# Moving four accumulations into x forward in the gated end stage of a transformer trunk, and one weight split ahead of a product's gating

## The chip, the cores and the metric

The kernel runs on one core of one Trainium2 chip. The metric is device time in microseconds (us) of one execution; the median over the runs shown is what counts.

## The reference, cut to what matters

One layer (DEPTH is 1, so the mixer is the sliding-window attention) on x of 512 rows and 2048 columns, all in float32:

```python
hn = rmsnorm(x, norm_g[i])
y = swa_mixer(hn, swa_w_in[j], swa_w_out[j], swa_sinks[j], rel_bias)   # ends in (out * silu(gate)) @ w_out
x = x + y
emb = p[i] @ ple_proj[i]
g = jax.nn.sigmoid(rmsnorm(x, ple_norm[i]) @ ple_gate[i])
x = x + emb * g
...
return rmsnorm(x, final_g)
```

The change lies in the last four lines: the product with `ple_gate` (2048 x 2048), the sigmoid, the update of x, and the final norm of each row.

## The kernel before

A float32 product is made of three matmuls in the fast float32 format (`mm3`): each operand is split into a high part (a cast on ScalarE, ACT) and a low part (a subtraction on VectorE, DVE). For the weights of `ple_gate` the cast is `bhi` (L755) and the subtraction `blo` (L756), each over a block of 128 x 1024; for the other operand they are `fhg` (L865) and `flg` (L866). ACT and DVE split two blocks ahead of TensorE (PE), and room for the split parts is reused, so that a split also waits for PE to have finished an older block.

The product with `ple_gate` is cut into halves of rows and of columns and made with seven smaller products instead of eight, numbered 1 to 7. Six of them run in the order 1, 7, 6, 5, 3, 4 (`ORDER_PLE`); product 2 is itself made by smaller ones (`Small`). Each of the six goes over two column blocks jj = 0, 1, and each of those over four weight blocks m = 0 to 3 (`unit`); a block is 12 matmuls with 512 columns. Behind each block `some_later` issues part of a list of postponed steps (`later`), and `todo` issues what a table gives for that place, named (product, jj, block). The order on every engine in this stage is the order in which the code issues (manual schedule for PE, SP, DVE, ACT and POOL), and each engine takes its instructions strictly in that order.

Weights reach SBUF in two ways. Plain blocks `braw` are loaded by the SyncE queue (SP). The blocks of products 7, 6 and 4 share eight tiles `grown`: loaded for product 7, then twice added to in place by a DMA that accumulates, from the GpSimd queue (POOL, L734). `Pieces.get` sets when such an addition is issued: its place is entered in `due`, and before the change this was 2 weight blocks behind the use by product 7 and 6 behind the use by product 6. Product 4's eight blocks are split into their own tiles, `last` (ACT, L763) and `low` (DVE, L764), by `split_last(k)`, k = 0 to 7.

Once a sum of products is complete for a quarter of the output, it is gated (`gated`): ACT makes `s` = sigmoid(rstd * z) (L1387), DVE multiplies by the embedding `e` (L1389), the result is added to `x1s` (the 512 x 2048 x, as column blocks j of 512 and row blocks t of 128), and ACT sums the squares of the new x for the norm (L1406). For t < 2 with j < 2 (the first quarter, its values in tile `s1`) and for t >= 2 with j >= 2 (values in `s7`) the addition is a DMA that accumulates, on POOL's queue (L1393); elsewhere it is an addition on DVE (L1395). `gate_later` puts these steps on `later`; for the first quarter the four DMAs go to the list `moves` and the squares to `moved`, and the lists are emptied into `later` at set places.

Behind the fifth product (3), whose second half is gated as `two`, comes the sixth (4) as four `block`s; their PSUM banks are filled beforehand with a copy from `s2` (`open_bank`, L1480). Rows 0 to 255 are then complete: DVE sums the squares (L1599), POOL makes the root (L1361), and rows are scaled by it and by `fg`, the final gain (`row` on DVE, L1424, or a scaling on ACT, L1432, on values that `by_gain`, L1416, has multiplied before), and stored by SP. Row blocks 2 and 3 follow in the same way.

Of the kernel before, what the change touches and what calls it, by code (L numbers as in the profile page):

```python
# [55 lines left out]
def trunk_kernel(ctx: ExitStack, tc: tile.TileContext, a: dict):  # L56
    nc = tc.nc
# [24 lines left out]
    def bank(name, tag):  # L82
        return others.get(tag, psum).tile([P, 512], F32, tag=tag, name=name)
# [4 lines left out]
    class Weights:  # L88
# [24 lines left out]
        def get(self, i):  # L113
            while self.asked <= min(i + self.ahead, len(self.srcs) - 1):
                self.todo.append(partial_of(self._make, self.asked))
                self.asked += 1
            while self.todo and not (self.apart and i < len(self.made)):
                self.todo.pop(0)()
            return self.made[i]
# [38 lines left out]
    def run(gen):  # L158
        for _ in gen:
            pass  # L160
# [21 lines left out]
    kinds, g = [], 0  # L182
# [16 lines left out]
    for k in range(KC):  # L199
# [67 lines left out]
        f, e = k == 0, k == KC - 1  # L267
# [27 lines left out]
        if 3 <= k < 3 + NB:  # L295
            t = k - 3
# [104 lines left out]
    for b in range(exact, BUCKETS):  # L401
        d = np.nonzero(bk == b)[0]
        if len(d):
            lo, n = P - 1 + int(d.min()), len(d)
# [296 lines left out]
    for nm, p in SUMS:  # L701
        for q in (6, 5) if (nm, p) == ("ple_gate", 5) else (p,):
            sum_small(nm, q)
        for jj in range(2):
            for m in range(4):
                t = summed[nm, p, jj, m] = tc.dram_tile([P, WE], F32, name=f"{nm}_{p}_{jj}_{m}")
# [13 lines left out]
    class Pieces:  # L720
# [59 lines left out]
        def get(self, i):  # L780
            self.ahead(i)

            key = self.specs[i][2]
            if key is not None:
                n = next((n for n in range(i + 1, len(self.specs)) if self.specs[n][2] == key), None)
                if n is not None:
                    self.due.append((i + (2 if self.specs[i][0] == "seed" else 6), n))
                    self.due.sort()
            while self.due and self.due[0][0] <= i:
                self._prepare(self.due.pop(0)[1])  # L790
            return self.made.pop(i)
# [177 lines left out]
    x1 = [x1s[:, j] for j in range(4)]  # L969
# [15 lines left out]
    later = []  # L985
# [6 lines left out]
    def unit(p, jj, at, forms, todo, between=lambda m, ps: None):  # L992

        ps = banks(p, jj, forms.nm)
        f = forms.made[p]
        first = p not in (6, 5, 3)
        for m in range(4):
            bh, bl = B.get(at[p, jj][m])
            for kk in range(2):
                k = 2 * m + kk  # L1000
                fh, fl = f[m]
                for tb in range(2):
                    mm3(ps[tb], fh[:, kk, blk(tb)], fl[:, kk, blk(tb)], bh[kk], bl[kk], first and k == 0, k == 7, not first)
            some_later(4 - m)
            todo()
            between(m, ps)
        return ps
# [297 lines left out]
    for n, p in enumerate(ORDER_OUT):  # L1305
        nxt = out_forms.steps(ORDER_OUT[n + 1]) if n < 5 else iter(())
        for jj in range(2):
# [28 lines left out]
            ps = unit(p, jj, at_out, out_forms, todo, between)  # L1336
# [32 lines left out]
    def load_embeds(c, jj):  # L1369
        t = embed_of[c, jj] = late.tile([P, 2, 512], F32, tag="e", name=f"e{c}_{jj}", bufs=2)  # L1370
        nc.sync.dma_start(t, embeds[c, jj])
# [40 lines left out]
    def gain(j):  # L1412
        return fg[:, j * 512 : (j + 1) * 512]

    def by_gain(t, j):
        nc.vector.tensor_mul(x1[j][:, t, :], x1[j][:, t, :], gain(j))  # L1416

    def store(t, j):
        nc.sync.dma_start(a["out"][t * P : (t + 1) * P, j * 512 : (j + 1) * 512], x1[j][:, t, :])

    def row(t, j, yn):

        xt = x1[j][:, t, :]
        nc.vector.scalar_tensor_tensor(out=xt, in0=xt, scalar=yn, in1=gain(j), op0=ALU.mult, op1=ALU.mult)  # L1424

    def rows_out(t):

        for j in (2, 3):
            row(t, j, yn2[:, t : t + 1])
            store(t, j)  # L1430
        for j in range(2):
            nc.scalar.mul(x1[j][:, t, :], x1[j][:, t, :], yn2[:, t : t + 1])  # L1432
            store(t, j)

    turns = [(kp, 1) for kp in range(4)]

    def gate(p, jj, ps, e):

        zs = []
        for tb in range(2):  # L1440
            v1, v2, v7 = s1[:, jj, tb], s2[:, jj, tb], s7[:, jj, tb]
            if p == 1:
                nc.scalar.mul(v1, ps[tb], -1.0)
            elif p == 7:
                (nc.vector.tensor_copy if tb else nc.scalar.copy)(v7, ps[tb])
            elif p == 6:
                nc.vector.tensor_add(v2, ps[tb], v7)
            elif p == 5:
                nc.vector.tensor_add(v7, ps[tb], v7)
                zs.append((2 + tb, 2 + jj, v7, v7))  # L1450
            elif p == 3:
                zs.append((tb, 2 + jj, ps[tb], v1))
            else:
                zs.append((tb, jj, v1, v1))
        return [gated(*z, e[z[0]]) for z in zs]
# [11 lines left out]
    moved, moves = [], []  # L1467
# [9 lines left out]
    def open_bank(jj, tb, tag, c=slice(0, 512)):  # L1477

        ps = opened[jj, tb, c.start] = bank(f"open{jj}_{tb}_{c.start}", tag)
        nc.scalar.mul(ps[:, c], s2[:, jj, tb, c], -1.0)  # L1480
# [24 lines left out]
    for n, p in enumerate(ORDER_PLE[:-1]):  # L1505
        if n == 1:

            ctx.enter_context(
                tc.manual_schedule(
                    engines={getattr(mybir.EngineType, v) for v in ("PE", "SP", "DVE", "Activation", "Pool")}  # L1510
                )
            )
        nxt = ple_forms.steps(ORDER_PLE[n + 1])
        for jj in range(2):
            calls = iter(range(4))

            def todo():
                step = next(calls)
                k = early.get((p, jj, step))
                if (p, jj, step) in embed_loads:  # L1520
                    load_embeds(*embed_loads[p, jj, step])
                while small_due:
                    small_due.pop(0)()
                if turns:
                    turn(*turns.pop(0), "t")
                    if not turns:
                        nc.vector.tensor_reduce(ss2, ssq2, axis=AX.X, op=ALU.add)
                        run(power_of_mean(rstd2, ss2, "r2"))
                        nc.scalar.activation(ss2[:, :1], ss2[:, :1], AF.Sigmoid)
                    return  # L1530
                next(nxt, None)
                if p == 1:
                    next(nxt, None)
                if k is not None:
                    split_last(k)
                if (p, jj, step) in opens:
                    open_bank(*opens[p, jj, step])
                if (p, jj, step) in gains:
                    by_gain(*gains[p, jj, step])

            def between(m, ps):
                if (p, m) == (7, 3):
                    gate(p, jj, ps, None)
                q = ple_steps.get((p, jj, m))
                if q is not None:
                    small_ple.prepare(q)
                for q in SMALL["ple_gate"].get((p, jj), {}).get(m, ()):
                    small_ple.product(q)
                if (p, jj, m) == (6, 1, 1):
                    later.append(partial_of(gate_later, "sum", 0, None, embeds_for(1, 0)))  # L1550

            ps = unit(p, jj, at_ple, ple_forms, todo, between)
            last_two, held_e = (p, jj) == (3, 1), {}
            if not (p == 7 or last_two):
                later.insert(0, partial_of(gate_later, p, jj, ps, held_e))
            for of, which in EMBEDS.get((p, jj), ()):
                e = embeds_for(of, which)
                held_e.update(e)
                if of == 1:
                    later.insert(1, partial_of(gate_later, "sum", which, None, dict(e)))  # L1560
                    held_e.clear()
            if (p, jj) == (5, 0):
                later.extend(moves)
            elif (p, jj) in ((5, 1), (3, 0)):
                while moved:
                    later.extend(moved.pop(0))
        run(nxt)
# [16 lines left out]
        return gated(2 + tb, jj, ps[:, c], s2[:, jj, tb, c], embed_of[4, jj][:, tb], c, share)  # L1584


    two = gate(3, 1, ps, e)
    for g in two:
        next(g)
    for g in two:  # L1590
        next(g)
    load_embeds(4, 1)
    split_last(7)
    open_bank(1, 1, "s", upper)
    for g in two:
        run(g)
    yn2 = const.tile([P, 3], F32, name="yn2")
# [5 lines left out]
    g = block(0, 0)  # L1603
    run(root)
    next(g)
    next(g)
    rows_out(0)
    run(g)
    g = block(1, 0)
    next(g)  # L1610
    next(g)
    rows_out(1)
    for j in (2, 3):
        by_gain(2, j)
    run(g)
    nc.vector.tensor_reduce(ssum[:, 2:], ssq3[:, 2, :4], axis=AX.X, op=ALU.add)
    root = power_of_mean(yn2[:, 2:], ssum[:, 2:], "r4")
    next(root)
    run(root)
    for j in range(2):  # L1620
        row(2, j, yn2[:, 2:])
        store(2, j)
# [3 lines left out]
    g = block(0, 1)  # L1626
    next(g)
    next(g)
    for j in (2, 3):
        by_gain(3, j)  # L1630
    run(g)
    by_gain(3, 0)

# [1 line left out]
    g = block(1, 1, lower)  # L1635
# [3 lines left out]
    n = done[3]  # L1639
# [81 lines left out]
```

## Time and profile before

| what | value |
| --- | --- |
| median of 3 runs (lowest to highest) | 799.19 us (798.86 to 799.58) |
| profiled execution: its time, its span | 799.52 us, 797.8 us |
| PE busy | 780.2 us, 98% of the span |
| DVE busy | 613.8 us, 77% |
| ACT busy | 525.5 us, 66% |
| POOL busy | 147.3 us, 18% |
| last matmul begins | 786.14 us |
| last product's DVE work on the result begins | 787.72 us |

Times inside the execution count from the start of the span. In a row of the timeline stand start, duration, engine, line, operation, output and input, a count where several in a row were merged, and in brackets how long the engine had stood idle before and what released it.

### The profile page before, as it was taken

The page shows a single profiled execution, that of the slowest core. Times are in us where ns is not written, and L with a number is a line of the kernel's source. Part 1 is how long each engine was busy: PE and PEld are TensorE (multiplying, and loading weights), DVE is VectorE, ACT ScalarE, POOL GpSimd, SP SyncE. Part 2 cuts the span into 40 slices and gives each one's busy share as a digit, 9 for nine tenths or more (in the row PEclk, how much of TensorE's full clock was granted, in tenths as well). Part 3 has the DMA queues.
Part 4 walks back from the last instruction along what each step waited for, and adds up shares of the span by engine and source line. Part 5 has one row for each costly group of instructions (what it writes and reads, how often), then busy time and mean ns, then how long its engine had stood idle before and what let it go on. Part 6 is the DMA issues. An engine that isn't in the chain of part 4 may idle for free. (4 is left out here: it accounts for less than half of the span.)

```text
span 797.8 us, 11160 instructions
## 1 busy us (share of the span) xinstructions
PE 780.2 (98%) x3708; PEld 651.0 (82%) x3708; DVE 613.8 (77%) x1054; ACT 525.5 (66%) x1103; POOL 147.3 (18%) x270
## 2 busy tenths in 40 slices
PE   9999999999999999999999999999999999999794
PEld 8888888888888888888888888888888888888573
DVE  4556697867877697777767998877887779988676
ACT  6752677666866677666666645667778966656773
POOL 0201423140322223141222100110000012212000
PEclk9999999999999999999999999999999999999897
DMA  9988999999999989999988499776894499997725
GB/s 350 283 225 270 210 287 299 277 290 246 294 280 273 259 227 297 249 313 232 307 240 187 162 351 335 232 223 241 310 354 163 165 334 275 272 302 235 211 73 192
DMA packets 49961, 205.94 MB, mean 258 GB/s; under 512 B 7456, under 2 KB 8480, under 8 KB 44144
## 3 DMA queue, kind: packets, MB, share of 16 engines
q1 hardware_dynamic: 39152, 154.58, 54.9%
q0 software_dynamic: 10752, 50.66, 31.4%
q8 instruction: 29, 0.48, 0.2%
q14 instruction: 28, 0.23, 0.1%
HBM read 192.31 MB, written 75.55 MB: 336 GB/s over the span
## 5 line engine op out<-in xcount | busy, mean ns | idle before, releaser
L756 DVE TENSOR_TENSOR blo<-braw,bhi 128x1024 fp32r<-128x1024 f32 x100 | 121.7, 1221 | 29.7 <-ACT bhi L755 29.0
L755 ACT CAST bhi<-braw 128x1024 fp32r<-128x1024 f32 x100 | 104.8, 1049 | 38.7 <-PE o L128 13.5
L126 PE MATMUL gps<-xh,whi 128*128 128x512 f32 x256 | 100.0, 390 | 0.0
L127 PE MATMUL gps<-xl,whi 128*128 128x512 f32 x256 | 99.9, 390 | 0.0
L128 PE MATMUL gps<-xh,wlo 128*128 128x512 f32 x256 | 99.7, 390 | 0.0
L126 PE MATMUL qps<-xh,whi 128*128 128x512 f32 x224 | 87.8, 392 | 0.0
L127 PE MATMUL qps<-xl,whi 128*128 128x512 f32 x224 | 87.4, 390 | 0.0
L128 PE MATMUL qps<-xh,wlo 128*128 128x512 f32 x224 | 87.3, 390 | 0.0
L570 POOL TENSOR_SCALAR_AFFINE_SELECT own<-r 64x512 fp32r<-64x512 f32 (+1 forms) x48 | 32.5, 677 | 243.4 <-DVE r L560 239.4
L110 DVE TENSOR_TENSOR wlo<-wraw,whi 128x1024 fp32r<-128x1024 f32 x60 | 73.5, 1226 | 2.8 <-ACT whi L109 2.7
L127 PE MATMUL o<-blo,fho 128*128 128x512 f32 x192 | 74.9, 390 | 0.0
L126 PE MATMUL o<-bhi,fho 128*128 128x512 f32 x192 | 74.8, 390 | 0.0
L128 PE MATMUL o<-bhi,flo 128*128 128x512 f32 x192 | 74.8, 389 | 0.0
L556 ACT CAST r<-pt 128x256 fp32r<-128x256 f32 x64 | 23.9, 374 | 69.0 <-PE pt L551 68.8
L126 PE MATMUL g<-bhi,fhg 128*128 128x512 f32 x160 | 63.8, 399 | 3.6 <-ACT bhi L755 3.6
L109 ACT CAST whi<-wraw 128x1024 fp32r<-128x1024 f32 x60 | 62.3, 1039 | 4.6 <-issue 4.1
L127 PE MATMUL g<-blo,fhg 128*128 128x512 f32 x160 | 63.9, 399 | 0.9 <-DVE blo L756 0.9
L128 PE MATMUL g<-bhi,flg 128*128 128x512 f32 x160 | 63.4, 396 | 0.0
L128 PEld LDWEIGHTS gps<-xh,wlo 128*128 128x128 f32 x256 | 48.1, 188 | 10.3
L126 PEld LDWEIGHTS gps<-xh,whi 128*128 128x128 f32 x256 | 48.1, 188 | 9.1
L529 ACT ACTIVATE t<-t,sm 128x129 f32<-128x129 f32 (+1 forms) x128 | 49.6, 389 | 8.7 <-DVE sm L525 7.3
L560 DVE TENSOR_TENSOR r<-pt,r 128x256 fp32r<-128x256 f32 x56 | 23.7, 423 | 41.1 <-ACT r L556 40.4
(290 smaller groups left out, 1834.2 us busy)
## 6 DMA issues: line engine op xcount, KB each, us to landing
wraw<-in_w_gate_in SPq DMA_DIRECT2D x32, 512.0 KB, 7.9
w_out<-in_w_out POOLq DMA_DIRECT2D x32, 512.0 KB, 8.9
braw<-w_out SPq DMA_DIRECT2D x32, 512.0 KB, 5.6
wraw<-in_w_q SPq DMA_DIRECT2D x28, 512.0 KB, 6.4
braw<-in_w_out SPq DMA_DIRECT2D x22, 512.0 KB, 4.7
braw<-in_ple_gate SPq DMA_DIRECT2D x22, 512.0 KB, 7.0
xw<-in_first SPq DMA_DIRECT2D x14, 640.5 KB, 6.7
w_out<-in_w_out SPq DMA_DIRECT2D x16, 512.0 KB, 10.3
```

What stands on the lines that cost most here:

```text
L109: nc.scalar.copy(hi, raw)
L110: nc.vector.tensor_sub(lo, raw, hi.bitcast(F32))
L126: nc.tensor.matmul(ps, sh, mh, start=first, stop=False, skip_group_check=more)
L127: nc.tensor.matmul(ps, sh, ml, start=False, stop=False, skip_group_check=more)
L128: nc.tensor.matmul(ps, sl, mh, start=False, stop=last, skip_group_check=more)
L529: nc.scalar.activation(su, su, AF.Exp, bias=sm[:, u : u + 1], accum_out=sm[:, 2 + u : 3 + u])
L556: nc.scalar.copy(rh, src)
L560: nc.vector.tensor_sub(rl, src, rh.bitcast(F32))
L570: nc.gpsimd.affine_select(out=flat(own), in_=flat(r).bitcast(F32), pattern=[[0, 8], [sign, HB]], compare_op=ALU.is_ge, fill=0.0, base=-HB ...
L755: nc.scalar.copy(hi[:, :n], raw)
L756: nc.vector.tensor_sub(lo[:, :n], raw, hi[:, :n].bitcast(F32))
```

## The change

Three things are moved; no arithmetic is added or removed.

- The four accumulating DMAs of the first quarter (`moves`) are issued at place (5, 0, 2), inside the first half of product 5, and no longer from `later` behind that half. So that all additions to `grown` are issued before that place, their distance behind product 6 is 3 blocks and no longer 6. The squares of the first quarter go on `later` one unit earlier, since the list is emptied behind every half of product 5.
- `split_last(7)` and the last `open_bank` stand ahead of the gating of the second half of product 3 (`two`); the load of an embedding (`load_embeds(4, 1)`) stays behind the multiplications of `two`.
- `rows_out` is written out: the four `row`s of row blocks 0 and 1 follow each other, and the square of block (0, 0) stands among the scalings on ACT; of the multiplications `by_gain` of row blocks 2 and 3, those of j = 2, 3 stand earlier.

```diff
--- before.py
+++ after.py
@@ -784,7 +784,7 @@
             if key is not None:
                 n = next((n for n in range(i + 1, len(self.specs)) if self.specs[n][2] == key), None)
                 if n is not None:
-                    self.due.append((i + (2 if self.specs[i][0] == "seed" else 6), n))
+                    self.due.append((i + (2 if self.specs[i][0] == "seed" else 3), n))
                     self.due.sort()
             while self.due and self.due[0][0] <= i:
                 self._prepare(self.due.pop(0)[1])
@@ -1423,15 +1423,6 @@
         xt = x1[j][:, t, :]
         nc.vector.scalar_tensor_tensor(out=xt, in0=xt, scalar=yn, in1=gain(j), op0=ALU.mult, op1=ALU.mult)
 
-    def rows_out(t):
-
-        for j in (2, 3):
-            row(t, j, yn2[:, t : t + 1])
-            store(t, j)
-        for j in range(2):
-            nc.scalar.mul(x1[j][:, t, :], x1[j][:, t, :], yn2[:, t : t + 1])
-            store(t, j)
-
     turns = [(kp, 1) for kp in range(4)]
 
     def gate(p, jj, ps, e):
@@ -1521,6 +1512,10 @@
                     load_embeds(*embed_loads[p, jj, step])
                 while small_due:
                     small_due.pop(0)()
+                if (p, jj, step) == (5, 0, 2):
+                    assert len(moves) == 4
+                    while moves:
+                        moves.pop(0)()
                 if turns:
                     turn(*turns.pop(0), "t")
                     if not turns:
@@ -1559,9 +1554,7 @@
                 if of == 1:
                     later.insert(1, partial_of(gate_later, "sum", which, None, dict(e)))
                     held_e.clear()
-            if (p, jj) == (5, 0):
-                later.extend(moves)
-            elif (p, jj) in ((5, 1), (3, 0)):
+            if p == 5 or (p, jj) == (3, 0):
                 while moved:
                     later.extend(moved.pop(0))
         run(nxt)
@@ -1584,14 +1577,13 @@
         return gated(2 + tb, jj, ps[:, c], s2[:, jj, tb, c], embed_of[4, jj][:, tb], c, share)
 
 
-    two = gate(3, 1, ps, e)
-    for g in two:
-        next(g)
-    for g in two:
-        next(g)
-    load_embeds(4, 1)
     split_last(7)
     open_bank(1, 1, "s", upper)
+    two = gate(3, 1, ps, e)
+    for _ in range(2):
+        for g in two:
+            next(g)
+    load_embeds(4, 1)
     for g in two:
         run(g)
     yn2 = const.tile([P, 3], F32, name="yn2")
@@ -1604,19 +1596,27 @@
     run(root)
     next(g)
     next(g)
-    rows_out(0)
-    run(g)
+    for t in range(2):
+        for j in (2, 3):
+            row(t, j, yn2[:, t : t + 1])
+            store(t, j)
+        for j in range(2):
+            nc.scalar.mul(x1[j][:, t, :], x1[j][:, t, :], yn2[:, t : t + 1])
+            store(t, j)
+            if t == j == 0:
+                run(g)
+    for j in (2, 3):
+        by_gain(2, j)
     g = block(1, 0)
     next(g)
     next(g)
-    rows_out(1)
-    for j in (2, 3):
-        by_gain(2, j)
+    by_gain(3, 2)
     run(g)
     nc.vector.tensor_reduce(ssum[:, 2:], ssq3[:, 2, :4], axis=AX.X, op=ALU.add)
     root = power_of_mean(yn2[:, 2:], ssum[:, 2:], "r4")
     next(root)
     run(root)
+    by_gain(3, 3)
     for j in range(2):
         row(2, j, yn2[:, 2:])
         store(2, j)
@@ -1626,8 +1626,6 @@
     g = block(0, 1)
     next(g)
     next(g)
-    for j in (2, 3):
-        by_gain(3, j)
     run(g)
     by_gain(3, 0)
```

## The prediction

> **What bounds the kernel now.** PE is busy for 98% of the span, so I first asked the waits for what PE stood still on. Columns: total us, times, longest.
>
> ```profile
> PE g L126 <- ACT bhi L755: 3.6, 1, 3.6
> PE g L127 <- DVE blo L756: 0.9, 1, 0.9
> PE open L127 <- DVE low L764: 0.8, 1, 0.8
> ```
>
> There are three gaps, 5.3 us together, all in the last 50 us. The timeline of PE places the first two, and the busy times by stretches (PE, PEld, DVE, ACT, POOL, then the granted clock) show what followed.
>
> ```profile
> 750.65 0.50 PE L126 MATMUL g<-bhi,fhg 128*128 128x512 f32 x1 [3.61 <-ACT bhi L755]
> 752.10 0.80 PE L127 MATMUL g<-blo,fhg 128*128 128x512 f32 x1 [0.95 <-DVE blo L756]
> ...
> 680.00:700.00 20.00, 20.00 (x90) 16.53 (x90) 19.17 (x22) 13.07 (x16) 4.77 (x6) 1.00 1.05 278
> ...
> 751.00:757.80 6.80, 5.85 (x14) 4.47 (x14) 5.61 (x6) 6.80 (x14) 0.00 (x0) 0.52 0.26 61
> ```
>
> At full clock 90 matmuls take 20 us, a block of 12 thus 2.7 us, and DVE is busy for 19.2 of these 20. Behind the gap the clock is granted at 0.52 for 6.8 us, so PE loses 6.8 x 0.48 = 3.3 us more. ACT's timeline says why the cast came late.
>
> ```profile
> 740.40 1.05 ACT L755 CAST bhi<-braw 128x1024 fp32r<-128x1024 f32 x1
> 742.26 0.63 ACT L1406 ACTIVATE s<-x1s 128x512 f32<-128x512 f32 x1 [0.82 <-DMA x1s<-s]
> ...
> 744.92 0.63 ACT L1406 ACTIVATE s<-x1s 128x512 f32<-128x512 f32 x1 [1.93 <-DMA x1s<-s]
> ...
> 747.48 0.63 ACT L1406 ACTIVATE s<-x1s 128x512 f32<-128x512 f32 x1 [1.84 <-DMA x1s<-s]
> ...
> 748.11 0.60 ACT L865 CAST fhg<-hT 128x512 fp32r<-128x512 f32 x1
> ...
> 749.56 1.04 ACT L755 CAST bhi<-braw 128x1024 fp32r<-128x1024 f32 x1
> ...
> 751.13 0.61 ACT L1406 ACTIVATE s<-x1s 128x512 f32<-128x512 f32 x1
> ...
> 751.75 0.61 ACT L1406 ACTIVATE s<-x1s 128x512 f32<-128x512 f32 x1
> ```
>
> Three squares of the first quarter wait 4.6 us for their accumulations, and the cast that PE needs is queued behind them. (The last two rows give a square's pitch: 0.62 us.) DVE stands still with ACT; its groups from 735 us to the end:
>
> ```profile
> L764 DVE TENSOR_TENSOR low<-grown,last 128x1024 fp32r<-128x1024 f32 x8 | 9.8, 1223 | 3.4 <-ACT last L763 3.4
> L1389 DVE TENSOR_TENSOR s<-e,s 128x512 f32<-128x512 f32 x9 | 6.1, 687 | 1.7 <-ACT s L1387 1.7
> L1416 DVE TENSOR_TENSOR x1s<-x1s,fg 128x512 f32<-128x512 f32 x9 | 5.9, 685 | 0.0
> L1395 DVE TENSOR_TENSOR x1s<-x1s,s 128x512 f32<-128x512 f32 x7 | 4.8, 692 | 0.2
> L866 DVE TENSOR_TENSOR flg<-hT,fhg 128x512 fp32r<-128x512 f32 x4 | 2.8, 691 | 6.6 <-ACT fhg L865 6.6
> ```
>
> Then the end of the chain:
>
> ```profile
> 773.54 0.16 DVE L1599 TENSOR_REDUCE ssum<-ssq 128x2 f32<-128x8 f32 x1
> ...
> 785.91 1.89 DVE L1416 TENSOR_TENSOR x1s<-x1s,fg 128x512 f32<-128x512 f32 x3
> 787.72 0.45 DVE L1389 TENSOR_TENSOR s<-e,s 128x288 f32<-128x288 f32 x1
> ...
> 786.14 0.27 PE L128 MATMUL open<-last,flg 128*128 128x224 f32 x1
> ```
>
> PE is done at 786.4, yet DVE takes up the last product's first part only at 787.72, directly behind other work. So from some point on DVE, not PE, sets the end, and from 787.72 the rest, 10.1 us to the end of the span, is one fixed chain.
>
> **The accumulations.** POOL's order before and in the change, from the last additions of weights (`grown`) on; `s1` are the values of the first quarter:
>
> ```order
> L734 DMA grown92_6960<-in_ple_gate 128x1024
> L734 DMA grown93_6975<-in_ple_gate 128x1024
> L1393 DMA x1s_5033<-s7_5038 128x512 x2
> L1393 DMA x1s_5033<-s1_5036 128x512 x4
> L1393 DMA x1s_5033<-s7_5038 128x512 x2
> ```
>
> ```order
> L734 DMA grown92_6960<-in_ple_gate 128x1024
> L734 DMA grown93_6975<-in_ple_gate 128x1024
> L1393 DMA x1s_5033<-s1_5036 128x512 x4
> L1393 DMA x1s_5033<-s7_5038 128x512 x4
> L1600 MEMSET power_6601 128x1
> ```
>
> The additions of weights keep their places, so the new distance of 3 changes no time; the four `s1` now stand ahead of the `s7`. What that gives is seen on POOL and DVE:
>
> ```profile
> 705.87 0.87 POOL L734 DMA_DIRECT2D grown<-in_ple_gate  x1 [1.46 <-DVE blo L756]
> 731.54 5.33 POOL L1393 DMA_DIRECT2D x1s<-s  x6 [24.80 <-DVE s L1389]
> ...
> 709.45 1.29 DVE L1389 TENSOR_TENSOR s<-e,s 128x512 f32<-128x512 f32 x2
> ...
> 722.74 1.29 DVE L1389 TENSOR_TENSOR s<-e,s 128x512 f32<-128x512 f32 x2
> 730.29 1.29 DVE L1389 TENSOR_TENSOR s<-e,s 128x512 f32<-128x512 f32 x2
> ...
> grown<-in_ple_gate POOLq DMA_DIRECT2D x5, 512.0 KB, 9.9
> ```
>
> POOL stood 24.8 us waiting for the `s7` multiplied at 730.29, while the `s1` were multiplied at 709.45 and 722.74. Now the first two go out at 710.8, and queue behind the last addition of weights, which by the median of 9.9 us lands about 715.8. The second two go out at about 721.5 (DVE multiplies them one low part and one split earlier than before, ACT's values allowing). How long they take, and what they do to the loads of weights, I take from two stretches: loads alone (q1), and both kinds together over 12 us.
>
> ```profile
> DMA packets 114, 0.42 MB, mean 418 GB/s; under 512 B 12, under 2 KB 12, under 8 KB 114
> ...
> q0 software_dynamic: 670, 1.24, 58.8%
> q1 hardware_dynamic: 614, 2.21, 49.0%
> ...
> DMA to landing us min/median/max: 3.8/11.3/15.8
> ```
>
> Together an accumulation of 256 KB takes 12 x 0.262 / 1.24 = 2.5 us and a load of 512 KB 12 x 0.524 / 2.21 = 2.8 us; alone a load takes 0.524 / 0.418 = 1.25 us. So the first pair lands about 718.4 and 720.9, and the second, by the least of 3.8 us and by the median of 11.3, between 725 and 733; I take 727, near the least, since nothing is queued ahead. ACT reaches the squares here:
>
> ```order
> L755 CAST bhi117_7519<-braw117_7463 128x1024
> L1406 ACTIVATE s1_5036,ssq3_5035<-x1s_5033 128x512 x2
> L755 CAST bhi118_7539<-braw118_7488 128x1024
> L1406 ACTIVATE s1_5036,ssq3_5035<-x1s_5033 128x512 x2
> L755 CAST bhi119_7559<-braw119_7517 128x1024
> ```
>
> ```profile
> 730.15 1.99 ACT L755 CAST bhi<-braw 128x1024 fp32r<-128x1024 f32 x2
> 733.25 1.05 ACT L755 CAST bhi<-braw 128x1024 fp32r<-128x1024 f32 x1 [1.11 <-PE g L128]
> ...
> 732.10 3.49 DVE L756 TENSOR_TENSOR blo<-braw,bhi 128x1024 fp32r<-128x1024 f32 x3
> ```
>
> These three casts are blocks 117 to 119; squares now stand behind each of the first two, at about 731 and 733, after both pairs have landed. The wait of 4.6 us goes. The four squares, 4 x 0.62 = 2.5 us, are not free: 1.1 us fall into ACT's idle time, and with the order of the steps around them block 119's subtraction, at 734.4 before (732.10 + 2 x 1.14), begins 0.6 us later.
>
> **The loads that the accumulations now meet.** Each of the four stretches a load from 1.25 to 2.8 us, in a stretch where ACT waited for loads already. ACT's two waits there, and DVE's split of block 115, which is the fourth load behind that of block 112 (113, 114, an embedding, 115):
>
> ```profile
> 712.02 1.05 ACT L755 CAST bhi<-braw 128x1024 fp32r<-128x1024 f32 x1 [1.03 <-DMA braw<-ple_gate]
> 715.83 1.05 ACT L755 CAST bhi<-braw 128x1024 fp32r<-128x1024 f32 x1 [2.76 <-DMA braw<-ple_gate]
> ...
> 725.08 1.22 DVE L756 TENSOR_TENSOR blo<-braw,bhi 128x1024 fp32r<-128x1024 f32 x1
> ```
>
> Block 112 landed at 715.8. If all four next loads go at the stretched pace, block 115 lands at 715.8 + 4 x 2.8 = 727.0, and its two splits (1.05 and 1.22) end at 729.3 and not at 726.3: 3.0 us late. If they go alone as now, 0. Between the pairs there is a pause: 113 and 114 at 2.8 land at 721.4, the embedding alone at 722.7, and 115 half beside the second pair at about 724.7, split by 727.0. I charge 1.0 us, with the bounds of 0 and 3.0. PE itself stands still for none of these three, or for less than 1 us: splits run two blocks (2 x 2.7 us) ahead. The Trainium skill's page "DMA: Bandwidth & Descriptors" (section "Queues, rings and completion order") says that each engine serves the queues that have work in turn, packet by packet. The stretch above agrees (2.5 us beside 2.8 us); the rule by itself, without the pause, would charge the upper bound and give rival B's time.
>
> **DVE's new sum.** So block 119's subtraction begins at 734.4 + 0.6 + 1.0 = 736.0. From there to the reduction DVE took 773.54 - 734.4 = 39.1 us, of which 6.6 + 3.4 = 10.0 were idle (rows above); eight gaps also cost the overlap of 1.22 - 1.14 = 0.08 each, 0.6 in all. The work is thus 28.5 us, the same instructions in another order. Three waits remain or are new: 1.9 us for `last5`, which ACT casts behind a square of the preceding half (0.82 with its read, then 0.95), 1.1 for `last6` behind an `open` and two squares, 0.9 for the last square ahead of the reduction. Reduction: 736.0 + 28.5 + 3.9 = 768.4, against 773.54: 5.1 us earlier. PE isn't late there: without gaps and the slow clock it would end 8.6 us earlier, at 777.8, and the last block is wanted at 781.
>
> The 0.8 us at `low7` goes too, since DVE has it now ahead of the gating:
>
> ```order
> L764 TENSOR_TENSOR low6_7758<-grown92_6960,last6_7757 128x1024
> L1416 TENSOR_TENSOR x1s_5033<-x1s_5033,fg_6241 128x512
> L764 TENSOR_TENSOR low7_7764<-grown93_6975,last6_7757 128x1024
> L1389 TENSOR_TENSOR s1_5036<-e3_1_7710,s1_5036 128x512
> L1395 TENSOR_TENSOR x1s_5033<-x1s_5033,s1_5036 128x512
> ```
>
> Four gating steps stood between these two `low` before. That gain is PE's and lies under DVE's sum: nothing more. **The tail:** from the reduction to 787.72 DVE took 14.2 us. Two of the three `by_gain` at 785.91 (0.6 us each) now stand ahead, but the remaining one waits for ACT's square of the same values (0.9 us), and the two moved ones stand in the chain ahead of the second root: by the same steps 13.9 us, 0.3 less, with bounds of -0.5 and +1.2.
>
> Sum: 5.1 + 0.3 = 5.4 us. The profiled execution took 799.52 us, of which the span is 797.8, so 794.1; it lies 0.3 above the median of 799.19, so the forecast is 799.19 - 5.4 = **793.8 us**. With the loads at their bounds (+1.0, -2.0) and the tail at its own (+0.9, -0.8) the case runs from 791.9 to 796.6.
>
> **Rivals.** A, PE is the bound after all: 3.6 + 0.95 + 3.3 + 0.8 = 8.6 us come back, 790.6. For it speaks PE's 98%; against it that DVE's idle time up to the reduction is 10 us and only the waits on squares go. 0.08.
>
> B, the loads are stretched without a pause: the charge is 3.0 us and not 1.0, the gain 3.4, the time 795.8. For it: the loads of 711 to 716 were late already. 0.18.
>
> C, slower: the accumulations hold the loads of blocks 113 to 115 back altogether, 4 x 2.5 = 10 us, less one block's time by which block 115 is early now (2.7). Block 119 then begins 7.3 us late; without any charge the gain is 6.4, so the kernel is 0.9 us slower, 800.1 us. It decides from a charge of 6.4 us on; from about 3 us PE stands still too, and the clock may fall again. Against it: loads went on at 2.8 us beside accumulations. The skill's page "TensorE: Matmul & The Clock Gate" (section "What's actually happening") puts the fall at an idle window of about 3.4 us; the gap of 3.61 us agrees, and by that rule only this rival brings it back. 0.07.
>
> D, the wait moves: the `s7` squares or the embeddings behind the moved steps stop ACT for as long as the `s1` did, and the time stays near 798.9. 0.05.
>
> **How the numbers follow.** The forecast has 0.62. A measurement of this kernel can tell about 0.2%, 1.6 us. Faster: 0.62 + 0.18 + 0.08 = 0.88; same 0.05; slower 0.07. The range 790.8 to 797.0 holds the forecast's own range and B, and leaves out C, D and the half of A that is below it.
>
> **What would show it.** The waits on `DMA x1s<-s` (4.6 us) and PE's gap of 3.6 us gone, the granted clock 1.00 through 751 to 758, PE done about 778, `low7`'s gap gone, DVE's reduction near 768 and its multiplication of 288 columns near 782. ACT waiting for `braw` between 716 and 730 for more than 3 us, or PE gaps there, would make B or C right; a reduction near 765 would make A right; a new wait for `s7` or `e` over 3 us, D.

## The result and the profile after

| what | before | after |
| --- | --- | --- |
| median of 6 runs each (lowest to highest) | 799.57 us (798.86 to 800.84) | 794.14 us (793.10 to 794.34) |
| ratio | | 0.9929, 95% interval 0.9916 to 0.9941 |
| profiled execution: its time, its span | 799.52, 797.8 us | 794.34, 792.6 us |
| DVE's reduction begins | 773.54 | 768.47 (forecast 768.4) |
| DVE's 288-column multiplication begins | 787.72 | 782.58 (forecast about 782) |

The change makes the kernel 5.4 us faster; the forecast was 793.8 us. The same views as before, now of the changed kernel. First the waits of PE, whole span; the third column of numbers is the longest.

```profile
PE warm_ps L141 <- PEq L1709: 0.8, 1, 0.8
PE qps L277 <- ACT xh L230: 0.2, 1, 0.2
```

The three gaps of the last 50 us are gone; what is left lies at the start of the kernel. In the busy times by stretches the clock that had been 0.52 is now full, and PE's last matmul in its timeline starts 8.2 us earlier (786.14 before):

```profile
751.00:757.80 6.80, 6.80 (x31) 5.40 (x30) 6.57 (x9) 3.09 (x7) 0.00 (x0) 1.00 0.00 0
```

```profile
777.98 0.27 PE L128 MATMUL open<-last,flg 128*128 128x224 f32 x1
```

Before, POOL stood for 24.8 us in front of an accumulation of `s7`, with the four moved ones queued behind it. Now its timeline shows the four in two pairs, straight behind the values that they add:

```profile
710.78 1.77 POOL L1393 DMA_DIRECT2D x1s<-s  x2 [3.95 <-DVE s L1389]
722.36 1.76 POOL L1393 DMA_DIRECT2D x1s<-s  x2 [9.81 <-PE g L128]
```

ACT's timeline: the four squares of the first quarter start without a wait (no bracket). Ahead of them ACT waits for weights, four times in this stretch:

```profile
712.48 1.05 ACT L755 CAST bhi<-braw 128x1024 fp32r<-128x1024 f32 x1 [1.39 <-DMA braw<-ple_gate]
716.27 1.05 ACT L755 CAST bhi<-braw 128x1024 fp32r<-128x1024 f32 x1 [2.74 <-DMA braw<-ple_gate]
...
718.91 1.05 ACT L755 CAST bhi<-braw 128x1024 fp32r<-128x1024 f32 x1 [0.54 <-DMA braw<-ple_gate]
...
723.91 1.05 ACT L755 CAST bhi<-braw 128x1024 fp32r<-128x1024 f32 x1 [1.25 <-DMA braw<-ple_gate]
...
731.24 0.62 ACT L1406 ACTIVATE s<-x1s 128x512 f32<-128x512 f32 x1
...
734.04 0.62 ACT L1406 ACTIVATE s<-x1s 128x512 f32<-128x512 f32 x1
```

DVE's timeline, the chain of the forecast: the subtraction of block 119, one more wait for a block, the two waits for `last5` and `last6`, the reduction with its wait for the last square, and the multiplication of 288 columns.

```profile
735.73 1.23 DVE L756 TENSOR_TENSOR blo<-braw,bhi 128x1024 fp32r<-128x1024 f32 x1 [0.95 <-ACT bhi L755]
...
742.20 1.23 DVE L756 TENSOR_TENSOR blo<-braw,bhi 128x1024 fp32r<-128x1024 f32 x1 [0.57 <-ACT bhi L755]
...
759.37 1.23 DVE L764 TENSOR_TENSOR low<-grown,last 128x1024 fp32r<-128x1024 f32 x1 [1.73 <-ACT last L763]
...
762.06 1.23 DVE L764 TENSOR_TENSOR low<-grown,last 128x1024 fp32r<-128x1024 f32 x1 [0.87 <-ACT last L763]
...
768.47 0.16 DVE L1591 TENSOR_REDUCE ssum<-ssq 128x2 f32<-128x8 f32 x1 [0.79 <-ACT s L1406]
...
769.05 0.69 DVE L1389 TENSOR_TENSOR s<-e,s 128x512 f32<-128x512 f32 x1
...
782.58 0.45 DVE L1389 TENSOR_TENSOR s<-e,s 128x288 f32<-128x288 f32 x1
```

PE is done at 778.25, and DVE takes up the last product's first part 4.3 us later. PE got 8.2 us back and the kernel 5.4. All that agrees with the forecast's sum, but one sum agreeing with one time does not show its terms. The experiments take them one by one.

### The profile page after: what moved, and what is told of

It is laid out like the page before. It is cut to its first block, busy times and chain, and to the rows that moved or that the text cites. A ratio compares the mean times of both kernels' runs of the same rounds, so it can differ in the third digit from the quotient of the medians.

```text
span 792.6 us, 11161 instructions
## 1 busy us (share of the span) xinstructions
PE 777.1 (98%) x3708; PEld 648.8 (82%) x3708; DVE 614.0 (77%) x1054; ACT 525.2 (66%) x1103; POOL 147.3 (19%) x270
```

## The experiments

Theory 1 is the prediction's: DVE's order, fed by ACT, sets the end from about 735 us on. Theory 2 is rival A in its general form: PE, with its gaps and its slow clock, sets it. Theory 3 is that each of the change's three parts has a share in the gain. The runs were made in groups, in which the kernel before had medians of 799.5 to 800.0; medians of two groups are compared with that in mind, and each ratio is against the kernel before of its own group. Work far ahead of every edit, such as ACT's cast at about 707 us, lies up to 1 us apart between profiles (707.22 to 708.21), so where a place in the program is compared between two kernels I count from that cast.

### The three parts, each alone

**The accumulations alone.** Edit, on the kernel before (with the squares one unit earlier, as in the change):

```diff
-self.due.append((i + (2 if self.specs[i][0] == "seed" else 6), n))
+self.due.append((i + (2 if self.specs[i][0] == "seed" else 3), n))
...
+                if (p, jj, step) == (5, 0, 2):
+                    assert len(moves) == 4
+                    while moves:
+                        moves.pop(0)()
...
```

> Only the moved accumulations (with their distance of 3 and the squares one unit earlier); low7, the last open and the tail stand as before. Theory 1 (the order of work on DVE and ACT sets the end from about 735 us on): nearly the whole gain comes from this part, 5.1 of the 5.3 us, so about 794.4 us where before is 799.4; the reduction stands within 0.5 us of 768.5 although PE waits again for low7, now about 1.9 us. Theory 2 (PE, with its gaps and its slow clock, sets the end): the 1.9 us at low7 show in full, about 796.0.

Measured: 792.82 us, ratio 0.9918 (0.9906 to 0.9931). This is 6.7 us faster than before, and by the medians 1.3 us faster than the whole change (the intervals overlap). So this part carries the gain, and more than theory 1 gave it. DVE's reduction begins at 766.72, without a wait, 1.8 us ahead of the place that was expected. PE's waits behind 690 us show one gap:

```profile
PE open L127 <- DVE low L764: 1.8, 1, 1.8
```

Theory 2 fails: with PE waiting 1.8 us for `low7` it expected 796.0 us, and the time is 3.2 us below that.

**`low7` alone.** Edit, on the kernel before:

```diff
+    split_last(7)
+    open_bank(1, 1, "s", upper)
     two = gate(3, 1, ps, e)
...
-    split_last(7)
-    open_bank(1, 1, "s", upper)
```

> Only split_last(7) and the last open_bank ahead of the gating; the accumulations and the tail stand as before. Theory 1: PE's wait of 0.8 us for low7 goes, but the end does not move: 799.4 us (within 0.2). Theory 2: 0.8 us less, 798.6.

Measured: 800.22 us, ratio 1.0011 (1.0003 to 1.0019): 0.7 us slower. Both theories missed it. PE's wait of 0.8 us is gone, as both had said, but DVE lost something. Its timeline here, from `last6`'s subtraction over the first reduction to the 288 columns:

```profile
768.05 1.23 DVE L764 TENSOR_TENSOR low<-grown,last 128x1024 fp32r<-128x1024 f32 x1 [0.87 <-ACT last L763]
...
774.46 0.16 DVE L1598 TENSOR_REDUCE ssum<-ssq 128x2 f32<-128x8 f32 x1 [0.79 <-ACT s L1406]
...
775.03 0.70 DVE L1389 TENSOR_TENSOR s<-e,s 128x512 f32<-128x512 f32 x1
...
788.24 0.45 DVE L1389 TENSOR_TENSOR s<-e,s 128x288 f32<-128x288 f32 x1
```

In the kernel before, `low7`'s subtraction stood between the last addition to x and the reduction, and ACT made the last square under it: the reduction at 773.54 had no wait. The rows of DVE and of ACT there, in the kernel before:

```profile
772.40 1.22 DVE L764 TENSOR_TENSOR low<-grown,last 128x1024 fp32r<-128x1024 f32 x1
```

```profile
772.52 0.63 ACT L1406 ACTIVATE s<-x1s 128x512 f32<-128x512 f32 x1 [0.60 <-DVE x1s L1395]
```

Moved ahead, the subtraction takes as long as before, but DVE then stands still for 0.79 us until the square is there.

**The tail alone.** Edit, on the kernel before: `rows_out` written out with the square of block (0, 0) among the scalings, and the `by_gain` of row blocks 2 and 3 as in the change.

> Only the new order of the tail (rows, square and multiplications by the gain); all else as before. Theory 1: the tail from the reduction to the 288-column multiplication is 0.3 us shorter, 799.1 us, between 798.2 (the moved multiplications by the gain are all hidden) and 799.9 (they lengthen the chain ahead of the second root). Theory 3 (each of the three parts is needed, and the tail's order is worth about 1 us by itself): 798.4 or less. By the trace of the changed kernel, where that stretch took 14.1 us and not 14.2, 799.3.

Measured: 799.45 us, ratio 0.9998 (0.9989 to 1.0007), not to be told from no change. Theory 3 fails with this: alone, `low7` loses and the tail shows no gain in the time. DVE's timeline gives the size that the time can't:

```profile
767.26 1.22 DVE L764 TENSOR_TENSOR low<-grown,last 128x1024 fp32r<-128x1024 f32 x1 [0.87 <-ACT last L763]
...
772.80 0.15 DVE L1590 TENSOR_REDUCE ssum<-ssq 128x2 f32<-128x8 f32 x1
...
773.16 0.69 DVE L1389 TENSOR_TENSOR s<-e,s 128x512 f32<-128x512 f32 x1
...
786.71 0.45 DVE L1389 TENSOR_TENSOR s<-e,s 128x288 f32<-128x288 f32 x1
```

From reduction to multiplication are 13.9 us, where the kernel before takes 14.2: the 0.3 us of the forecast. In the whole change it was 14.1, since `low7` ahead of the gating also makes ACT's next sigmoid late: the multiplication behind the reduction begins 0.58 us after it (768.47 to 769.05) and not 0.36, as here (772.80 to 773.16).

### Which engine sets the end

One DVE instruction more, and twelve matmuls more (which add some terms of one block's sum a second time), each on the changed kernel:

```diff
-            nc.vector.tensor_sub(lo, raw, hi.bitcast(F32))
+            for _ in range(2 if k == 3 else 1):
+                nc.vector.tensor_sub(lo, raw, hi.bitcast(F32))
```

> The changed kernel with one instruction more on DVE: the subtraction that makes low3 (128x1024), at about 750 us, is done twice with the same result. Theory 1 (DVE's order sets the end): one such subtraction follows the other every 1.14 us, so 1.1 us more, 795.2. Theory 2 (PE sets the end): DVE is two blocks ahead, no change, 794.1.

```diff
-        for k in range(8):
+        for k in (0, 1, 2, 3, 0, 1, 2, 3, 4, 5, 6, 7) if (jj, tb) == (0, 0) else range(8):
```

> The changed kernel with 12 matmuls more at the start of the sixth product: the first four k of block (0,0) are multiplied twice, so that this block's sum holds these terms twice. At 20 us for 90 matmuls that is 2.7 us of PE. Theory 1: PE, done at 778.2 where the last part is taken up at 782.6, has room for it; the first blocks' gating at about 770 comes later by 2.7 us, but PE is ahead of DVE there too: 794.1 to 795.0. Theory 2: the whole 2.7 us, 796.8.

Measured: with the DVE instruction 795.27 us (ratio 0.9946, 0.9934 to 0.9959), 1.13 us more than the changed kernel's 794.14; the intervals overlap, the single runs do not (794.72 to 795.93, against 793.10 to 794.34). With the matmuls 793.54 us (0.9929, 0.9916 to 0.9943), no more. The first row is the doubled subtraction in DVE's timeline of the first kernel; the two rows after it are PE's last matmul and DVE's multiplication in the second:

```profile
750.32 2.48 DVE L765 TENSOR_TENSOR low<-grown,last 128x1024 fp32r<-128x1024 f32 x2
```

```profile
779.86 0.27 PE L128 MATMUL open<-last,flg 128*128 128x224 f32 x1
```

```profile
781.74 0.45 DVE L1389 TENSOR_TENSOR s<-e,s 128x288 f32<-128x288 f32 x1
```

One instruction more on DVE (2.48 us for the two) costs 1.13 us of time; matmuls of 2.7 us on PE cost nothing, though PE's end moved by 1.9 us, from 778.25 to 780.13. The timelines agree: from block 119's subtraction to the multiplication of 288 columns it takes 47.45 us with the DVE instruction (736.43 to 783.88) and 46.20 with the matmuls (735.54 to 781.74). The DVE instruction also makes PE wait, 1.0 us for `blo`; that this is not what it costs is seen from the matmuls, where PE ends later still and the time does not move. PE is busy for 98% of the span and DVE for 77%, and yet theory 1 holds for the changed kernel, in this stretch.

### What the accumulations cost beside the loads

```diff
-            nc.gpsimd.dma_start(xt, z, accum_op=ALU.add)
+            if t >= 2:
+                nc.gpsimd.dma_start(xt, z, accum_op=ALU.add)
```

> The changed kernel without the four accumulations of the first quarter; the addition of these values to x is left out. Theory 1, with loads stretched by the accumulations (the prediction's charge of 1.0 us): ACT's waits for weights between 710 and 730 us return from 9.7 to about 8 us, block 119's subtraction begins about 1 us earlier, 793.1. If the loads lose nothing by them: 794.1. If they lose as rival B had it (3.0 us): 791.1.

This kernel leaves out the addition of the first quarter's values to x. Measured: 792.94 us, ratio 0.9916 (0.9902 to 0.9929), 1.2 us less than the changed kernel by the medians; the intervals overlap. ACT's waits from 705 to 735 us (total, times, longest), then the cast that I count from and block 119's subtraction, first of the changed kernel, then of this one:

```profile
ACT bhi L755 <- DMA braw<-ple_gate: 5.9, 4, 2.7
```

```profile
707.30 1.05 ACT L755 CAST bhi<-braw 128x1024 fp32r<-128x1024 f32 x1 [1.66 <-PE g L128]
```

```profile
ACT bhi L755 <- DMA braw<-ple_gate: 3.7, 2, 2.8
```

```profile
707.78 1.05 ACT L755 CAST bhi<-braw 128x1024 fp32r<-128x1024 f32 x1 [1.67 <-PE g L128]
```

```profile
735.09 1.23 DVE L756 TENSOR_TENSOR blo<-braw,bhi 128x1024 fp32r<-128x1024 f32 x1 [0.95 <-ACT bhi L755]
```

From the cast to the subtraction it takes 28.4 us with the accumulations (735.73 - 707.30) and 27.3 without (735.09 - 707.78): a charge of 1.1 us, where the forecast had 1.0 and rival B 3.0. One pair of profiles does not fix it so closely: the same stretch takes 28.5 us with the DVE instruction more, 28.3 with the matmuls more and 27.7 with the accumulations alone (707.78 to 735.51), and up to there these have the changed kernel's order. So the charge lies between 0.4 and 1.2 us, well below 3.0. The wait of 2.8 us stays without them, so it isn't theirs: the waits that they add are the small ones, 0.54 and 1.25 us at 718.9 and 723.9 and part of the 1.39 at 712.5.

### The distance of the weight additions

The changed kernel with `else 6` in place of `else 3`.

> The changed kernel with the distance of the last additions of weights back at 6: the last two of them stand behind the first and the second pair of accumulations on POOL. By the prediction the distance changes no time by itself: 794.1, within 0.5. If the last weight additions ahead of the first pair cost the loads or the squares something: 793.4 or less. If product 4's split then waits for the late addition: 795 or more.

Measured: 795.03 us, ratio 0.9939 (0.9926 to 0.9951), 0.9 us more by the medians; the intervals overlap. POOL's timeline and then ACT's and DVE's show how it would come about:

```profile
711.69 1.78 POOL L1393 DMA_DIRECT2D x1s<-s  x2 [10.34 <-DVE s L1389]
712.84 1.53 POOL L734 DMA_DIRECT2D grown<-in_ple_gate  x1
721.54 1.76 POOL L1393 DMA_DIRECT2D x1s<-s  x2 [7.18 <-DVE s L1389]
722.69 1.51 POOL L734 DMA_DIRECT2D grown<-in_ple_gate  x1
```

```profile
736.44 1.05 ACT L755 CAST bhi<-braw 128x1024 fp32r<-128x1024 f32 x1 [1.50 <-DMA braw<-in_ple_gate]
```

```profile
737.52 1.23 DVE L756 TENSOR_TENSOR blo<-braw,bhi 128x1024 fp32r<-128x1024 f32 x1 [2.56 <-ACT bhi L755]
```

With the old distance each of the last two additions of weights stands behind a pair of accumulations, the last one goes out at 722.7 in place of 706, and the load of block 119 comes late: ACT waits 1.50 us for it where the changed kernel doesn't, and from the cast to the subtraction it takes 29.3 us (708.21 to 737.52) in place of 28.4. That the addition is what delays this load is inferred from their places, not tried by itself.

### Toward a better version

Two experiments took up what theory 1 says is left: the squares' place on ACT, and DVE's waits for the casts of `last5` and `last6`. On the changed kernel, the first two squares go to the front of the list two blocks earlier:

```diff
+            if (p, jj) == (5, 0):
+                later[:0] = moved.pop(0)
```

> The changed kernel with the first two squares of the first quarter placed two blocks earlier on ACT, where it stands idle for 2.1 us (just ahead of 727 us); the other postponed steps move up one or two places in the list. Theory 1: 1.2 us of squares fall into idle time, block 119's subtraction begins about 1 us earlier, and the end comes 1 us earlier, 793.0. If something behind 735 us other than DVE's order sets the end: 794.1. If the first two accumulations have not landed by then, ACT waits for them, and it is slower: 795.

Measured: 792.51 us, ratio 0.9912 (0.9898 to 0.9925), 1.6 us less than the changed kernel; the intervals overlap, the single runs do not (at most 792.74, against 793.10 and more). The list hands out its steps by counts, so the other postponed steps moved too, and the 1.6 us belong to the whole new order.

For the casts, on the changed kernel, only through the second half of product 3:

```diff
-            some_later(4 - m)
-            todo()
+            if forms.nm == "g" and (p, jj) == (3, 1):
+                todo()
+                some_later(4 - m)
+            else:
+                some_later(4 - m)
+                todo()
```

> The changed kernel, but through the second half of product 3 the casts of last4 to last6, their subtractions and the opens are issued ahead of the postponed gating steps of the same place and not behind them. Theory 1: DVE's waits of 1.73 and 0.87 us for those casts go, and as DVE's order sets the end, up to 2.6 us come back: 791.5 us; at least 0.9 if the wait returns as a wait for the gating's values, 793.2. Theory 2 (PE sets the end since its gaps are gone): PE's work is untouched, 794.1.

Measured: 793.84 us, ratio 0.9932 (0.9920 to 0.9945): nothing. DVE's wait did not go, it only stands one block later, as ACT's timeline and DVE's show:

```profile
759.14 0.63 ACT L1410 ACTIVATE s<-x1s 128x512 f32<-128x512 f32 x1 [2.34 <-DVE x1s L1399]
...
759.77 1.04 ACT L763 CAST last<-grown 128x1024 fp32r<-128x1024 f32 x1
```

```profile
760.84 1.22 DVE L764 TENSOR_TENSOR low<-grown,last 128x1024 fp32r<-128x1024 f32 x1 [1.73 <-ACT last L763]
```

ACT stands in front of a square whose values DVE has yet to add, the cast is queued behind that square, and DVE then waits for the cast. Moving the cast and its subtraction together keeps this ring closed. So in the next kernels the cast alone goes ahead. First, the change with the early squares and with `low7` left where it stood before:

> The changed kernel with the first two squares earlier (as in sq_early) and without the move of low7 and the last open, so that it differs from sq_early (792.5 us) by that move alone. If low7's subtraction, standing behind the gating, covers ACT's last square ahead of the reduction (DVE's wait of 0.79 us and ACT's later sigmoid go), 0.8 us less: 791.7, though PE waits again 1.8 us for low7. If the move of low7 is worth nothing, as the prediction had it: 792.5. If PE's wait for low7 shows: 794.

Measured: 791.59 us, ratio 0.9897 (0.9882 to 0.9913), 0.9 us less than with the move of `low7`; the single runs of the two do not overlap (791.50 to 792.01, and 792.33 to 792.74). DVE's timeline with the move, then without it:

```profile
766.88 0.16 DVE L1593 TENSOR_REDUCE ssum<-ssq 128x2 f32<-128x8 f32 x1 [0.79 <-ACT s L1406]
```

```profile
764.81 1.22 DVE L764 TENSOR_TENSOR low<-grown,last 128x1024 fp32r<-128x1024 f32 x1
765.95 0.15 DVE L1594 TENSOR_REDUCE ssum<-ssq 128x2 f32<-128x8 f32 x1
```

PE waits 1.0 us for `low7` in the latter, and the kernel is still the faster one. Next, in it, the casts of `last5` to `last7` one place earlier, without their subtractions:

```diff
+        for n in {0: (0,), 2: (2,), 4: (4, 5), 5: (6,), 6: (7,)}.get(k, ()):
+            ...
+            if n >= 5:
+                B.split_last(n, ..., None)   # the cast alone
```

> As best1, with ACT's casts of last5, last6 and last7 issued one place earlier each, ahead of the squares that wait for DVE's additions; DVE's order is the same. Theory 1 (DVE sets the end): DVE's waits of 1.73 and 0.87 us for last5 and last6 go, 2.6 us less than best1: 789.1. Theory 2 (PE, done about 778, sets the end once DVE is 2.6 us earlier) or the waits move to the squares of the reduction: no less than 791.0.

Measured: 790.43 us, ratio 0.9883 (0.9869 to 0.9896), 1.2 us less than the kernel before it and not 2.6. Both waits for `last` are gone from DVE, but a new one has come, behind ACT's casts and squares:

```profile
761.57 0.69 DVE L1392 TENSOR_TENSOR s<-e,s 128x512 f32<-128x512 f32 x1 [1.79 <-ACT s L1390]
```

Last, ACT's two squares of the `s7` values behind these sigmoids (the list `moved` is then no longer emptied behind the first half of product 3):

```diff
...
+    while moved:
+        for step in moved.pop(0):
+            step()
...
```

> As best2, with ACT's last two squares of the s7 values behind the sigmoids of the second half of product 3 and no longer ahead of them, where in best2 DVE waits 1.79 us for these sigmoids. If ACT's order is what holds DVE there: the wait falls to 0.6 or less, 1.2 to 1.8 us less than best2's 790.4, 788.6 to 789.2. If PE (the end of product 3, or the blocks of product 4 behind it) has become the bound: the wait stays, as one for PE, 790.4.

Measured: 789.63 us, ratio 0.9874 (0.9858 to 0.9891), 0.8 us less by the medians (the single runs of the two just overlap, 790.28 and 790.20), short of the 1.2 to 1.8 expected. The wait for the sigmoids is gone; a smaller one has come for `last4`, which in this order is cast behind `last5`:

```profile
752.13 1.23 DVE L767 TENSOR_TENSOR low<-grown,last 128x1024 fp32r<-128x1024 f32 x1 [1.03 <-ACT last L763]
...
777.71 0.45 DVE L1392 TENSOR_TENSOR s<-e,s 128x288 f32<-128x288 f32 x1
```

PE's timeline ends with this row:

```profile
776.71 0.27 PE L128 MATMUL open<-last,flg 128*128 128x224 f32 x1
```

DVE's multiplication begins at 777.71, 0.7 us behind the end of PE's last matmul (776.71 + 0.27): PE's lead has shrunk from 4.3 us to 0.7. This version beats the changed kernel by 4.5 us and the one before by 1.26% (0.9874).

## Why the prediction was right, and where it was not

**The bound** was the step that carried it: not PE, busy for 98%, but DVE's order. It is shown by the two additions (1.13 us for one instruction of DVE, nothing for 2.7 us of PE). Rival A's 8.6 us did come back on PE (8.2) and ended as PE's lead over DVE.

**The accumulations.** The squares no longer wait, the clock stays full, and block 119's subtraction begins at 735.73 (forecast 736.0). The three waits that the sum kept, 1.9, 1.1 and 0.9 us, measured 1.73, 0.87 and 0.79. The reduction came within 0.1 us of the forecast, in part by luck: a further wait of 0.57 us for a block, which the sum has not, filled what these were short. It is missing in the profiles with the matmuls more and without the accumulations, where it takes 46.2 us from block 119's subtraction to the 288 columns and not 46.9 (735.73 to 782.58).

**The charge for the loads** of 1.0 us, chosen near the lower end of 0 to 3.0, measured 1.1, and 0.4 to 1.2 by the other profiles. My own sign for rivals B and C, over 3 us of ACT's waits for `braw` from 716 to 730, came true (2.74 + 0.54 + 1.25 = 4.5, with the wait that ends at 716.27 counted whole) without either rival: the kernel before had 2.76 of them in the same place already (ending at 715.83), so the sign should have been the difference.

**The distance of 3** was told rightly as far as it went: in the change the additions of weights keep their places. That it "changes no time by itself" is true only because of this; with the old distance they would have slid behind the moved accumulations, 0.9 us slower by the medians.

**`low7`: the step that failed.** "Nothing more", said the prediction, since PE's gain lies under DVE's sum. PE's gain does lie there, but the move costs DVE 0.87 us up to the reduction: from `last6`'s subtraction on that took 5.54 us before (768.00 to 773.54) and 6.41 with `low7` alone (768.05 to 774.46). Of the whole time it cost 0.7 us alone, and 0.9 in the kernel with the early squares. The price was in the sum, as the wait of 0.9 us ahead of the reduction, and I put it down as one of the accumulations' waits. So two terms were mis-assigned and the sum came out right: the accumulations are worth 6.7 us by the medians and not 5.1, and `low7` takes about 0.9 of it back. The same piece of work, standing where DVE would otherwise wait, is cover; I asked what PE gains from its going and not what it had covered on DVE.

**The tail** was 0.3 us by itself, as forecast, and 0.1 in the whole change, because of `low7`. The three parts alone sum to 6.7 - 0.7 + 0.1 = 6.1 us, the change gives 5.4; the interplay of `low7` and the tail in DVE's timelines explains about 0.6. DVE's timeline of before, from `last6`'s subtraction on (its end at 787.72 stands in the prediction):

```profile
768.00 1.23 DVE L764 TENSOR_TENSOR low<-grown,last 128x1024 fp32r<-128x1024 f32 x1 [0.87 <-ACT last L763]
...
777.77 0.69 DVE L1389 TENSOR_TENSOR s<-e,s 128x512 f32<-128x512 f32 x1 [1.12 <-ACT s L1387]
```

From there to the multiplication it takes 19.7 us before, 20.2 with `low7` alone (768.05 to 788.24), 19.4 with the tail alone (767.26 to 786.71) and 20.5 with both (762.06 to 782.58): +0.5, -0.3, and +0.8 together. In the old tail a wait of 1.12 us for a later sigmoid took up part of `low7`'s delay; the new tail has no wait there to take it up.

**Rival C** was far off: the accumulations did not hold the loads back, and PE did not wait once in the last 100 us. **Rival D** did not occur here, but later: with the waits for `last5` and `last6` removed, two thirds of them came back as a wait for the sigmoids.

## What to carry to other kernels

An engine at 98% can be ahead of the one that sets the end: look at which engine takes up the last result, and whether the value had been lying there. Before moving an instruction on the bounding engine, ask what latency of another engine it covers where it stands; and when two engines wait for each other in a ring, move only the link that opens it, since the pair moved together takes the wait along. Put an accumulating DMA on an in-order queue as soon as its values exist, ahead of any that waits for later values.

## What was not expected of the hardware

In the kernel with the new tail alone PE's gap came out shorter than before, and the clock fell all the same. PE's timeline, and the stretches with the granted clock as the third number from the end:

```profile
749.92 0.79 PE L126 MATMUL g<-bhi,fhg 128*128 128x512 f32 x1 [3.17 <-ACT bhi L755]
751.37 0.79 PE L127 MATMUL g<-blo,fhg 128*128 128x512 f32 x1 [0.66 <-DVE blo L756]
```

```profile
744.00:751.00 7.00, 3.55 (x14) 2.23 (x12) 2.74 (x3) 4.98 (x11) 0.00 (x0) 0.86 1.08 305
751.00:757.80 6.80, 6.43 (x19) 5.11 (x20) 5.60 (x7) 6.80 (x13) 0.00 (x0) 0.64 0.18 36
```

In stretches of 0.1 us the clock is granted at 0.50 from 749.1 to 755.9 here, and from 751.2 to 758.1 in the kernel before: 6.8 us each time. Here the fall came 2.3 us into the gap of 3.17 us; before, it came 0.6 us behind the end of the gap of 3.61 us, in the next one (of 0.95 us). The gap of 1.8 us in the kernel with the accumulations alone brought no fall (1.00 from 760 to 780 us). The Trainium skill's page "TensorE: Matmul & The Clock Gate" (section "What's actually happening") gives the idle window as about 3.4 us and free-running; this trace does not agree that a whole window of that length has to be idle, since a gap of 3.17 us was enough here. What share of a window has to be idle no run here shows.

Open: of the 1.3 us by which the accumulations alone beat the whole change, `low7` and the tail explain 0.8 in DVE's timelines. In the two profiles the rest lies in waits for loads, ahead of every place at which the orders of the two differ: up to block 119's subtraction the accumulations alone take 0.7 us less (27.7 against 28.4), and they have no wait of 0.57 us for a block behind it. Why the loads come at other times in the same order is not known.
